# Layer norm 2 normalized by one ScalarE pass, with its weight and bias applied behind the transposes

## The chip, the cores and the metric

The kernel runs on one core of one Trainium2 chip. The metric is the device time of one execution in microseconds (us), lower is better. The engines are named as in the profile: PE (TensorE, with its weight loads PEld), DVE (VectorE), ACT (ScalarE), POOL (GpSimd) and SP (SyncE, which here only issues weight transfers).

## The reference, cut to what matters

Two transformer blocks run one after the other on 256 tokens of width 1024, all in float32. The first block ends in a mixture of experts and a layer norm. The second is two layers of feed-forward, mixer, feed-forward. The change lies on the seam between them:

```python
        ffn = hier_moe(x, w_group[l], b_group[l], w_expert[l], b_expert[l], w_gate_up[l], w_down[l])
        x = layer_norm(DN_ALPHA * x + ffn, ln2_g[l], ln2_b[l])
...
        x = x + FFN_RES_WEIGHT * _swiglu(_rmsnorm(x, ffn1_norm[layer]),
                                         ffn1_w_gate_up[layer], ffn1_w_down[layer])
```

`layer_norm` subtracts each token's mean, multiplies by the reciprocal standard deviation, by the weight `ln2_g` and adds `ln2_b`. `_rmsnorm` divides by the root mean square and multiplies by the gain `ffn1_norm`. The mixer also needs two scalars "lambda", one a layer, each from two dot products of length 64 and an exponential.

## The kernel before, in words

Tokens lie in two tiles of 128 partitions, `t` = 0 and 1, each in two column halves of 512, `hf` = 0 and 1. The order on every engine is the order in which the code is written; an engine works through its list and waits at each instruction for what it needs.

**The experts.** 32 experts go in 8 groups of four (`q` = 0 to 7). SP streams their weights through 10 slots of 1 MB and some more buffers (`Stream`), always ahead of PE. Each group's result is added in PSUM into four banks `yacc[t][hf]`. In the last group `down` leaves `ys`, of which ACT copies one half and DVE the other, and `last` adds it into `yacc`. Between the last `gate_up` and `down` stands `overflow`, a conditional branch that is not entered for these inputs. `gains` (group 6) spreads rows of weights over 128 partitions with small PE products and ACT copies; `lambdas` (group 7) computes the two lambdas.

**LN2 before.** `last_stats(t)` takes `bn_stats` of both halves on DVE, `bn_aggr`, and on POOL the reciprocal standard deviation (L808, L809). `first_norm` then makes on DVE, in two passes over each half, the normalized row with the product of both gains (`ggb`) in it, into `s_xn`. PE transposes it, four 128x128 blocks to a PSUM bank `tp` (`trans_half`, L1362), and `split` makes the two parts that the products need: ACT copies `tp` to `XH` in a rounded format (L300), DVE subtracts to get the rest, `XL` (L301). ACT copies `yacc` to `X` (L1818), which DVE later normalizes with weight and bias for the residual (L813, L814).

**The first feed-forward.** Weights are split the same way by `Feeder`: ACT makes `whi` (L140), DVE `wlo` (L154), in pieces of 1024 columns, each good for two of the eight chunks `k` of the contraction. Every product is three matmuls (`mm3`: L295 with `whi` and `XH`, L296 with `wlo`, L297 with `XL`). The first block, `skew_first`, does token tile 0 (`part(0, k)`), with the transposes of tile 1 between, and then tile 1. From the second block on, a product is for both token tiles at once (256 columns; PSUM tiles `g`, `a`, `o`).

Of the kernel before, what the change touches and what calls it, by code (L numbers as in the profile page):

```python
# [180 lines left out]
def body(tc, A, out, taps=None, stop=None):  # L181
# [3 lines left out]
    with es:  # L185
# [993 lines left out]

        lam = const.tile([128, 2], F32, name="lam")  # L1180
# [8 lines left out]
        def gains():  # L1189
            for c, op in ((0, ALU.mult), (1024, ALU.add)):  # L1190
                for hf in range(2):
                    p = spread(s_ln[32:33, c + hf * 512:c + hf * 512 + 512], 32)
                    for t in range(2):
                        dve.tensor_tensor(X[:, t, hs(hf)], X[:, t, hs(hf)], p, op)
            for a, n in ((s_ln, 4), (s_gg, 2)):
                for i in range(n):
                    act(a[:, hs(i)], spread(a[0:1, hs(i)]), AF.Copy)
            act(aux[:, 512:1024], spread(aux[0:1, 512:1024]), AF.Copy)
            for c in (1, 0):
                pool.tensor_tensor(s_gg[:, c * 1024:(c + 1) * 1024], s_ln[:, c * 1024:(c + 1) * 1024],  # L1200
                                   s_gg[:, 0:1024], ALU.mult)
# [23 lines left out]
        for q in range(NQ):  # L1225
# [5 lines left out]
            def used(c):  # L1231
                for i in gu[c]:
                    st.done(i)
                if q in (CST, CST + 1) and c == 1:
                    st.reserve = 3
                if q == CST + 1 and c == 1:
                    gains()
                if tail and c == 1:
                    scatter(*prev, (0,))
# [11 lines left out]
            if tail:  # L1251
                lambdas()
                s_xn, sA, sB = [st.take() for _ in range(3)]
                overflow(s_xn, sA, sB)
                st.give(sA, sB)
            else:
                way_back(P, q + 1)
                gather(P, 0, q > CST)
# [4 lines left out]
            if q == CST:  # L1263
                s_ln, s_gg, aux = [st.take() for _ in range(3)]
                pool.dma_start(s_ln[0:1, 0:1024], A["ln2_g"])
                pool.dma_start(s_ln[0:1, 1024:2048], A["ln2_b"])
                pool.dma_start(s_ln[32:33, 0:1024], A["ln1_g"])
                pool.dma_start(s_ln[32:33, 1024:2048], A["ln1_b"])
                pool.dma_start(s_gg[0:1, 0:1024], A["ffn1_norm_2"][0:1])
                pool.dma_start(aux[:, 0:512], A["cossin"])  # L1270
                pool.dma_start(aux[0:1, 512:1024], A["lam"])
                pool.dma_start(wr[:, 0:128], A["w_ff"].rearrange("p l n -> p (l n)"))
                pool.dma_start(wr[:, 128:130], A["subln"])
                pool.dma_start(wr[0:8, 130:132], A["fbias"])
                fone = aux[0:8, 1792:2048]
# [4 lines left out]
        ggb = [s_gg[:, c * 1024:(c + 1) * 1024] for c in range(2)]  # L1280
# [10 lines left out]
        def first_norm(t, i):  # L1291

            for hf in range(2):
                dst = s_xn[:, t * 1024 + hf * 512:t * 1024 + (hf + 1) * 512]
                dve.scalar_tensor_tensor(dst, dst if i else yacc[t][hf], mvs[t][:, 3 * i:3 * i + 1],
                                         ggb[i][:, hs(hf)], op0=ALU.mult if i else ALU.subtract,
                                         op1=ALU.add if i else ALU.mult)
# [5 lines left out]
        for i in range(2):  # L1303
            first_norm(0, i)
# [52 lines left out]
        def trans_half(t, hf, src=None):  # L1357
            p = pa("tp")
            src = xn[t] if src is None else src
            for i in range(4):  # L1360
# [3 lines left out]
                  p.rearrange("p (c t) -> p c t", c=4))  # L1364

# [11 lines left out]
        def skew_first(banks, first=False):  # L1377
# [8 lines left out]
            for k in range(4):  # L1386
                part(0, k)
            trans_half(1, 0, xs_[1] if first else None)
            for k in range(4, 8):
                part(0, k)  # L1390
            trans_half(1, 1, xs_[1] if first else None)
            if first:
                for t in range(2):
                    normed(X[:, t], X[:, t], mvs[t], *lnb)
                    stats(t)
            else:
                stats(1)
# [47 lines left out]
        def ffn(g_next, keep_free, first=False, final=False):  # L1445
# [57 lines left out]
            for j in range(NJ):  # L1503
# [3 lines left out]
                if j == 0:  # L1507
                    skew_first(banks, first)
                    if first:
                        st.give(s_ln, s_xn, s_gg)  # L1510
# [294 lines left out]
        xs_ = [s_xn[:, t * 1024:(t + 1) * 1024] for t in range(2)]  # L1805
        fd.hold = True
        fd.hb = 4
        fd.fill()
        fd.flush(1)
        for hf in range(2):  # L1810
            trans_half(0, hf, xs_[0])
        mvs[1] = last_stats(1)
        fd.flush(1)
        for i in range(2):
            first_norm(1, i)
        for t in range(2):
            for hf in range(2):
                act(X[:, t, hs(hf)], yacc[t][hf], AF.Copy)  # L1818
# [17 lines left out]
def host(I):  # L1836
# [3 lines left out]
    A = {}  # L1840
# [37 lines left out]
    A["mrow"] = np.broadcast_to(np.where(dist >= 0, 0.0, -NEG).astype(f), (8, 384))  # L1878
    A["w_rt"] = np.concatenate([I["w_group"][0], I["w_expert"][0]], 1).reshape(8, 128, 36).transpose(1, 0, 2)
# [34 lines left out]
```

## Time and profile before

| | |
|---|---|
| median of 3 runs | 1664.7 us (1662.6 to 1664.9) |
| profiled execution | 1666.04 us, span of the trace 1664.3 us |
| PE busy | 1540.4 us, 93% of the span |
| DVE busy | 819.8 us, 49% |
| ACT busy | 657.3 us, 39% |
| POOL busy | 88.6 us, 5% |
| PE's share of the chain that ended last | 54% |
| mean granted TensorE clock | 0.971 |

The profiled execution lies 1.3 us above the median of the runs, and its span 1.7 us below its own time. Busy shares are averages over stages with different limits: the experts, up to some 665 us, move weights at over 420 GB/s, and behind some 690 us PE is busy nearly all the time. The seam between lies in the two rows of the profile's 40 slices where DMA and PE both have gaps.

### The profile page before, as it was taken

Reading aid. Unit: us, or ns where it says so; the run is one execution under the profiler, and the core shown is the slowest. Engines: PE = TensorE matmul, PEld = TensorE weight load, DVE = VectorE, ACT = ScalarE, POOL = GpSimd, SP = SyncE. Lnnn points to the kernel's source line nnn. Section 1 sums busy time; section 2 is a strip of 40 time slices with the busy share of each in tenths; the row PEclk is TensorE's granted clock in tenths of the full one; section 3 lists DMA queues with packets and bytes.
Section 4 is the critical chain, followed back from the end, with each engine's and each line's share of the span. In section 5 each row is a group of like instructions: output and inputs, shape, how many; then the busy total and the mean of one; then the engine's idle time right before and its main releaser. Section 6 shows DMA issues by size and latency. Waiting matters only on the chain.

```text
span 1664.3 us, 24689 instructions
## 1 busy us (share of the span) xinstructions
PE 1540.4 (93%) x10220; PEld 1201.7 (72%) x10220; DVE 819.8 (49%) x1251; ACT 657.3 (39%) x987; POOL 88.6 (5%) x135
## 2 busy tenths in 40 slices
PE   8999998687677896899999999999999999999998
PEld 7889963122122231699989879999999989889997
DVE  5875640000000100855567865556655568765555
ACT  5556420000000110544445654444544455654442
POOL 3010000000000010100002000000000020000000
PEclk9999999999998798999999999999999999999999
DMA  9757779999999999875614555555555514475500
GB/s 357 195 183 280 279 302 422 422 421 421 421 421 420 419 421 417 318 272 182 203 36 157 206 212 203 200 188 192 190 192 189 176 64 153 178 265 178 200 29 26
DMA packets 85764, 416.49 MB, mean 250 GB/s; under 512 B 7464, under 2 KB 7672, under 8 KB 50320
## 3 DMA queue, kind: packets, MB, share of 16 engines
q1 hardware_dynamic: 82688, 407.07, 64.2%
q0 software_dynamic: 2688, 6.75, 1.4%
q8 instruction: 82, 1.34, 0.3%
q10 hardware_dynamic: 272, 1.05, 0.2%
q14 instruction: 34, 0.28, 0.0%
HBM read 413.56 MB, written 1.25 MB: 249 GB/s over the span
## 4 chain that ended last, share of the span: by engine, by line
PE 54%; DVE 4%; ACT 1%; issue 0%; POOLq 0%; DVEq 0%; POOL 0%; ACTq 0%
PE g L297 8%; PE g L296 8%; PE g L295 8%; PE o L296 5%; PE o L295 5%; PE o L297 5%; PE a L295 4%; PE a L296 3%; PE a L297 3%; DVE wlo L154 1%; PE tp L1362 1%; PE ro L1612 0%; ACT whi L140 0%; PE t L1631 0%; PE fo L469 0%
## 5 line engine op out<-in xcount | busy, mean ns | idle before, releaser
L154 DVE TENSOR_TENSOR wlo<-slot,whi 128x1024 fp32r<-128x1024 f32 x274 | 330.8, 1223 | 202.8 <-ACT whi L140 202.5
L140 ACT ACTIVATE whi<-slot 128x1024 fp32r<-128x1024 f32 x274 | 284.6, 1055 | 223.5 <-PE o L296 69.9
L295 PE MATMUL o<-XH,whi 128*128 128x256 f32 x640 | 177.2, 277 | 0.0
L296 PE MATMUL o<-XL,whi 128*128 128x256 f32 x640 | 177.0, 276 | 0.0
L297 PE MATMUL o<-XH,wlo 128*128 128x256 f32 x640 | 176.9, 276 | 0.0
L295 PE MATMUL g<-whi,OH 128*128 128x512 f32 x416 | 165.2, 397 | 0.0
L297 PE MATMUL g<-whi,OL 128*128 128x512 f32 x416 | 163.9, 394 | 0.0
L296 PE MATMUL g<-wlo,OH 128*128 128x512 f32 x416 | 163.1, 392 | 0.0
L295 PE MATMUL a<-XH,whi 128*128 128x256 f32 x512 | 141.5, 276 | 0.0
L296 PE MATMUL a<-XL,whi 128*128 128x256 f32 x512 | 141.5, 276 | 0.0
L297 PE MATMUL a<-XH,wlo 128*128 128x256 f32 x512 | 141.4, 276 | 0.0
L1070 PE MATMUL eg<-slot,xe 128*32 128x512 f32 x232 | 97.8, 690 | 28.2 <-DMA slot<-in_w_gate_up_dram 28.2
L296 PEld LDWEIGHTS o<-XL,whi 128*128 128x128 f32 x640 | 120.4, 188 | 0.7
L295 PEld LDWEIGHTS o<-XH,whi 128*128 128x128 f32 x640 | 120.1, 188 | 0.7
L297 PEld LDWEIGHTS o<-XH,wlo 128*128 128x128 f32 x640 | 120.2, 188 | 0.0
L1074 DVE TENSOR_TENSOR eb<-eb,eu 128x512 f32<-128x512 f32 x8 | 5.5, 688 | 232.0 <-PE eu L1070 224.0
L295 PE MATMUL g<-XH,whi 128*128 128x256 f32 x384 | 113.9, 297 | 0.0
L297 PE MATMUL g<-XH,wlo 128*128 128x256 f32 x384 | 106.8, 278 | 0.0
L296 PE MATMUL g<-XL,whi 128*128 128x256 f32 x384 | 106.7, 278 | 0.0
L296 PEld LDWEIGHTS a<-XL,whi 128*128 128x128 f32 x512 | 96.2, 188 | 0.7
L295 PEld LDWEIGHTS a<-XH,whi 128*128 128x128 f32 x512 | 96.1, 188 | 0.7
L297 PEld LDWEIGHTS a<-XH,wlo 128*128 128x128 f32 x512 | 96.1, 188 | 0.0
(521 smaller groups left out, 3369.3 us busy)
## 6 DMA issues: line engine op xcount, KB each, us to landing
slot<-in_gu_dram SPq DMA_DIRECT2D x74, 1024.0 KB, 4.9
slot<-in_w_gate_up_dram SPq DMA_DIRECT2D x58, 1024.0 KB, 19.8
slot<-in_w_in_dram SPq DMA_DIRECT2D x36, 1024.0 KB, 5.1
slot<-in_dn_dram SPq DMA_DIRECT2D x34, 1024.0 KB, 4.9
ew<-in_w_down_dram SPq DMA_DIRECT2D x24, 1024.0 KB, 19.8
slot<-in_w_down_dram SPq DMA_DIRECT2D x21, 1024.0 KB, 19.8
ew<-in_w_gate_up_dram SPq DMA_DIRECT2D x16, 1024.0 KB, 19.8
m<-in_w_gate_up_dram SPq DMA_DIRECT2D x13, 1024.0 KB, 19.8
```

Of the source, the lines that this page charges most:

```text
L140: self.nc.scalar.activation(hi[:, c], src[:, c], AF.Copy)
L154: self.low.tensor_tensor(lo[:, c], src[:, c], hi.bitcast(F32)[:, c], ALU.subtract)
L295: mm(o, sh, mh, start=start, stop=False, skip_group_check=skip)
L296: mm(o, sh, ml, start=False, stop=False, skip_group_check=skip)
L297: mm(o, sl, mh, start=False, stop=stop, skip_group_check=skip)
L1070: mm(b[r, :], xe[:, k, r], get(k // 2, e)[:, c:c + 512], start=k == 0, stop=k == 7)
L1074: dve.tensor_tensor(esg, esg, u, ALU.mult)
L1362: nc.tensor.transpose(p[:, i * 128:(i + 1) * 128], src[:, c], ident)
```

## The change

It has five parts. The normalized row is made by ACT alone, from the bank in PSUM straight into `X`, with the reciprocal deviation as scale and minus mean times that as bias (`plain_norm2`; POOL computes the bias, L1293). PE transposes this plain `X`, and weight and bias of LN2, multiplied by the gain of the first RMS norm, are applied behind the transposes, where features lie on partitions (`turn_first`): ACT writes a 128x128 block of `XH`, DVE writes the same block in full to a buffer, four times in turn, and then DVE subtracts. The weights come as `lnc`, 24 columns, and `s_gg` and `s_xn` are gone. The residual's `X` gets weight and bias by plain `tensor_tensor` (L1407). `lambdas` is called from `gains`, one group earlier, and the reserve of slots follows. In `skew_first` the first transposes of tile 1 stand behind six chunks of tile 0 and no longer four; the weight splits are handed out in other steps (`fd.hb` 2, 3, 4).

```diff
-            for c in (1, 0):
-                pool.tensor_tensor(s_gg[:, c * 1024:(c + 1) * 1024], s_ln[:, c * 1024:(c + 1) * 1024],
-                                   s_gg[:, 0:1024], ALU.mult)
+            for c in (0, 8):
+                pool.tensor_tensor(lnc[:, c:c + 8], lnc[:, c:c + 8], lnc[:, 16:24], ALU.mult)
+            lambdas()
...
-                    st.reserve = 3
+                    st.reserve = 2 + q - CST
...
-                lambdas()
-                s_xn, sA, sB = [st.take() for _ in range(3)]
-                overflow(s_xn, sA, sB)
-                st.give(sA, sB)
+                sl = [st.take() for _ in range(3)]
+                overflow(*sl)
+                st.give(*sl)
...
-        def first_norm(t, i):
-
+        def plain_norm2(t):
+
+            mv = mvs[t]
+            pool.tensor_scalar(mv[:, 4:5], mv[:, 0:1], mv[:, 3:4], -1.0, op0=ALU.mult, op1=ALU.mult)
             for hf in range(2):
-                dst = s_xn[:, t * 1024 + hf * 512:t * 1024 + (hf + 1) * 512]
-                dve.scalar_tensor_tensor(dst, dst if i else yacc[t][hf], mvs[t][:, 3 * i:3 * i + 1],
-                                         ggb[i][:, hs(hf)], op0=ALU.mult if i else ALU.subtract,
-                                         op1=ALU.add if i else ALU.mult)
+                act(X[:, t, hs(hf)], yacc[t][hf], AF.Identity, scale=mv[:, 3:4], bias=mv[:, 4:5])
...
-        for i in range(2):
-            first_norm(0, i)
...
+        def turn_first(t, hf):
+
+            p, f = pa("tp"), xn[hf][:, 0:512]
+            for i in range(4):
+                c = 4 * hf + i
+                nc.tensor.transpose(p[:, i * 128:(i + 1) * 128], X[:, t, c * 128:(c + 1) * 128], ident)
+            for i in range(4):
+                c, b = 4 * hf + i, slice(i * 128, (i + 1) * 128)
+                g, b_ = lnc[:, c:c + 1], lnc[:, 8 + c:9 + c]
+                act(XH[:, c, tsl(t)], p[:, b], AF.Identity, scale=g, bias=b_)
+                dve.tensor_scalar(f[:, b], p[:, b], g, b_, op0=ALU.mult, op1=ALU.add)
+            d = slice(4 * hf, 4 * hf + 4)
+            dve.tensor_tensor(XL[:, d, tsl(t)], f.rearrange("p (c t) -> p c t", c=4), XH[:, d, tsl(t)].bitcast(F32),
+                              ALU.subtract)
...
-            for k in range(4):
+            turn = turn_first if first else trans_half
+            n = 6 if first else 4
+            for k in range(n):
                 part(0, k)
-            trans_half(1, 0, xs_[1] if first else None)
-            for k in range(4, 8):
+            turn(1, 0)
+            for k in range(n, 8):
                 part(0, k)
-            trans_half(1, 1, xs_[1] if first else None)
+            turn(1, 1)
             if first:
                 for t in range(2):
-                    normed(X[:, t], X[:, t], mvs[t], *lnb)
+                    for a, op in zip(lnb, (ALU.mult, ALU.add)):
+                        dve.tensor_tensor(X[:, t], X[:, t], a, op)
                     stats(t)
...
-        xs_ = [s_xn[:, t * 1024:(t + 1) * 1024] for t in range(2)]
         fd.hold = True
+        fd.hb = 2
+        fd.fill()
+        fd.flush()
+        plain_norm2(0)
+        turn_first(0, 0)
+        fd.hb = 3
+        fd.fill()
+        turn_first(0, 1)
+        fd.flush()
+        mvs[1] = last_stats(1)
+        plain_norm2(1)
         fd.hb = 4
         fd.fill()
-        fd.flush(1)
-        for hf in range(2):
-            trans_half(0, hf, xs_[0])
-        mvs[1] = last_stats(1)
-        fd.flush(1)
-        for i in range(2):
-            first_norm(1, i)
-        for t in range(2):
-            for hf in range(2):
-                act(X[:, t, hs(hf)], yacc[t][hf], AF.Copy)
         fd.flush()
```

Two places show how the lists of the engines move. First ACT, from the copy of `ys` after the last expert group to the sums of squares (`junk`), before:

```order
L977 ACT_TABLE_LOAD
L977 ACTIVATE ys<-ey 128x512
L140 ACTIVATE whi<-eXL 128x1024 x2
L140 ACTIVATE whi<-slot_69 128x1024 x2
L300 ACTIVATE XH<-tp 128x4x128 x2
L1818 ACTIVATE X<-yacc 128x512 x4
L140 ACTIVATE whi<-slot_70 128x1024 x2
L300 ACTIVATE XH<-tp 128x4x128 x2
L1374 ACTIVATE junk,ss<-X 128x1024 x2
```

and ACT at the same place in the changed kernel (`wr` holds `lnc`, `mv` the statistics):

```order
L977 ACTIVATE ys<-ey 128x512
L140 ACTIVATE whi<-eXL 128x1024 x2
L1295 ACTIVATE X<-yacc,mv 128x512 x2
L1370 ACTIVATE XH<-tp,wr 128x128 x4
L140 ACTIVATE whi<-slot_69 128x1024
L1370 ACTIVATE XH<-tp,wr 128x128 x4
L1295 ACTIVATE X<-yacc,mv 128x512 x2
L140 ACTIVATE whi<-slot_69 128x1024
L140 ACTIVATE whi<-slot_70 128x1024 x2
L1370 ACTIVATE XH<-tp,wr 128x128 x8
L1384 ACTIVATE junk,ss<-X 128x1024 x2
```

The table load ahead of `ys` is gone, `X` of tile 0 now stands ahead of `XH`, each `XH` half is four instructions in place of one, and three weight splits stand between `X` and `XH` of tile 1.

Then DVE, from the first statistics of LN2 to the last `XL` of tile 1, before:

```order
L1288 BN_STATS bst<-yacc 128x6 x2
L807 BN_AGGR mv<-bst 128x2
L1295 SCALAR_TENSOR_TENSOR slot_68<-yacc,mv,slot_72 128x512 x2
L1295 SCALAR_TENSOR_TENSOR slot_68<-slot_68,mv,slot_72 128x512 x2
L154 TENSOR_TENSOR wlo<-eXL,whi 128x1024
L301 TENSOR_TENSOR XL<-tp,XH 128x4x128 x2
```

and DVE at the same place in the changed kernel:

```order
L1287 BN_STATS bst<-yacc 128x6 x2
L807 BN_AGGR mv<-bst 128x2
L154 TENSOR_TENSOR wlo<-eXL,whi 128x1024 x2
L1371 TENSOR_SCALAR xn_3895<-tp,wr 128x128 x4
L1373 TENSOR_TENSOR XL<-xn_3895,XH 128x4x128
L1371 TENSOR_SCALAR xn_3896<-tp,wr 128x128 x4
L1373 TENSOR_TENSOR XL<-xn_3896,XH 128x4x128
L154 TENSOR_TENSOR wlo<-slot_69,whi 128x1024
```

Behind the statistics two weight splits stand at once where the two passes of `first_norm` stood, and each `XL` half now has four reads of the bank `tp` ahead of it; the statistics of tile 1 come a further split later.

## Rows read from the trace of the kernel before

**Rows 1.** Windows: busy time of each engine, granted clock (PEclk), DMA share, GB/s.
```profile
600.00:640.00 40.00, 32.01 (x212) 11.39 (x211) 2.35 (x7) 2.69 (x7) 0.00 (x0) 1.00 1.01 422
```

**Rows 2.** Waits, 692 to 860 us, the only one of PE: us, times, longest.
```profile
PE tp L1362 <- DVE xn L1355: 0.3, 1, 0.3
```

**Rows 3.** Chain that ended last, 666 to 692 us: start, duration, what.
```profile
672.92 1.22 DVE wlo L154
...
677.86 0.72 DVE slot L1295 x2
...
680.51 1.15 DVE wlo L154
```

**Rows 4.** Timeline, 665 to 677 us: start, duration, what, and the idle time before.
```profile
665.26 1.28 ACT L977 ACT_TABLE_LOAD   x1 [12.32 <-PE ey L1092]
...
666.55 0.60 ACT L977 ACTIVATE ys<-ey 128x512 f32<-128x512 f32 x1
...
667.20 3.70 PE L1284 MATMUL yacc<-ys,eb 128*128 128x512 f32 x8 [1.17 <-ACT ys L977]
...
669.96 0.21 DVE L807 BATCH_NORM_AGGREGATE mv<-bst 128x2 f32<-128x12 f32 x1
...
672.48 1.29 PE L1362 MATMUL tp<-cst,slot 128*128 128x128 f32 x8 [1.58 <-DVE slot L1295]
...
675.25 1.28 DVE L1288 BATCH_NORM_STATS2 bst<-yacc 128x6 f32<-128x512 f32 x2
```

**Rows 5.** Timeline of POOL over the whole span.
```profile
670.26 0.22 POOL L808 TENSOR_SCALAR mv<-mv 128x1 f32<-128x1 f32 x1 [81.60 <-DVE mv L807]
...
671.11 0.66 POOL L1332 DMA_DIRECT2D slot<-in_late_dram  x1
676.88 1.08 POOL L808 TENSOR_SCALAR mv<-mv 128x1 f32<-128x1 f32 x1 [5.11 <-DVE mv L807]
...
984.54 1.06 POOL L1369 TENSOR_TENSOR rs<-v,mhalf 128x1 f32<-128x1 f32 x1
```

**Rows 6.** Timeline of DVE, 984 to 986 us.
```profile
984.50 0.69 DVE L1355 TENSOR_TENSOR xn<-X,gain 128x512 f32<-128x512 f32 x1
985.16 1.22 DVE L154 TENSOR_TENSOR wlo<-eXH,whi 128x1024 fp32r<-128x1024 f32 x1
```

**Rows 7.** Timeline of ACT, 215 to 232 us: the plain norm of LN1.
```profile
226.23 1.52 ACT L872 ACTIVATE X<-X,mv 128x512 f32<-128x512 f32 x2 [1.12 <-POOL mv L870]
```

**Rows 8.** Timeline, 228 to 236 us: ACT and DVE in turn on one bank `ga`.
```profile
231.36 0.46 ACT L1006 ACTIVATE xe<-ga,bcol 128x128 f32<-128x128 f32 x1 [3.61 <-PE ga L993]
231.85 0.41 DVE L1004 TENSOR_SCALAR xe<-ga,bcol 128x128 f32<-128x128 f32 x1 [1.80 <-ACT xe L1006]
...
232.29 0.81 ACT L1006 ACTIVATE xe<-ga,bcol 128x128 f32<-128x128 f32 x2 [0.48 <-DVE xe L1004]
```

**Rows 9.** Groups of instructions, 665 to 720 us: count, busy us and mean ns, idle before.
```profile
L154 DVE TENSOR_TENSOR wlo<-slot,whi 128x1024 fp32r<-128x1024 f32 x12 | 13.9, 1220 | 2.3 <-ACT whi L140 2.2
L140 ACT ACTIVATE whi<-slot 128x1024 fp32r<-128x1024 f32 x12 | 11.9, 1049 | 0.3 <-PE g L296 0.3
```

**Rows 10.** Timeline of PE: the first feed-forward block, and the second's first matmul.
```profile
683.14 0.63 PE L296 MATMUL o<-wlo,XH 128*128 128x512 f32 x1
683.57 0.63 PE L297 MATMUL o<-whi,XL 128*128 128x512 f32 x1
...
691.86 0.39 PE L296 MATMUL o<-wlo,XH 128*128 128x512 f32 x1
692.09 0.39 PE L297 MATMUL o<-whi,XL 128*128 128x512 f32 x1
692.32 0.28 PE L295 MATMUL g<-XH,whi 128*128 128x256 f32 x1
```

**Rows 11.** Windows, as Rows 1, in which the granted clock was low.
```profile
679.60:686.20 6.60, 6.02 (x16) 4.58 (x17) 6.05 (x7) 2.60 (x4) 0.10 (x1) 0.51 1.02 407
```

**Rows 12.** Timeline of ACT, 583 to 594 us: first instruction behind `gains`.
```profile
593.98 0.60 ACT L1073 ACTIVATE eb<-eg 128x512 f32<-128x512 f32 x1 [8.48 <-PE eg L1070]
```

More of the change, by code (lines that the diff above doesn't have):

```diff
@@ L1178, in token_weights @@
                 dve.scalar_tensor_tensor(WW[:, t], A1[:, t], rw[:, t, 6:7], WW[:, t], op0=ALU.mult, op1=ALU.add)
+        lnc = wr[:, 260:284]
         lam = const.tile([128, 2], F32, name="lam")
@@ L1194, in gains @@
                         dve.tensor_tensor(X[:, t, hs(hf)], X[:, t, hs(hf)], p, op)
-            for a, n in ((s_ln, 4), (s_gg, 2)):
-                for i in range(n):
-                    act(a[:, hs(i)], spread(a[0:1, hs(i)]), AF.Copy)
+            for i in range(4):
+                act(s_ln[:, hs(i)], spread(s_ln[0:1, hs(i)]), AF.Copy)
             act(aux[:, 512:1024], spread(aux[0:1, 512:1024]), AF.Copy)
-            for c in (1, 0):
-                pool.tensor_tensor(s_gg[:, c * 1024:(c + 1) * 1024], s_ln[:, c * 1024:(c + 1) * 1024],
-                                   s_gg[:, 0:1024], ALU.mult)
+            for c in (0, 8):
+                pool.tensor_tensor(lnc[:, c:c + 8], lnc[:, c:c + 8], lnc[:, 16:24], ALU.mult)
+            lambdas()
         def lambdas():
@@ L1263, in body @@
             if q == CST:
-                s_ln, s_gg, aux = [st.take() for _ in range(3)]
+                s_ln, aux = [st.take() for _ in range(2)]
                 pool.dma_start(s_ln[0:1, 0:1024], A["ln2_g"])
@@ L1268, in body @@
                 pool.dma_start(s_ln[32:33, 1024:2048], A["ln1_b"])
-                pool.dma_start(s_gg[0:1, 0:1024], A["ffn1_norm_2"][0:1])
+                pool.dma_start(lnc, A["lnc"])
                 pool.dma_start(aux[:, 0:512], A["cossin"])
@@ L1279, in body @@
         lnb = [s_ln[:, c * 1024:(c + 1) * 1024] for c in range(2)]
-        ggb = [s_gg[:, c * 1024:(c + 1) * 1024] for c in range(2)]
         bsts = [small.tile([128, 12], F32, name="bst", bufs=2) for _ in range(2)]
@@ L1355, in finish, with trans_half @@
             dve.tensor_tensor(xn[t][:, hs(hf)], xs, g[:, hs(hf)], ALU.mult)
-        def trans_half(t, hf, src=None):
-            p = pa("tp")
-            src = xn[t] if src is None else src
+        def trans_half(t, hf):
+            p, src = pa("tp"), xn[t]
             for i in range(4):
@@ L1364, in trans_half @@
                   p.rearrange("p (c t) -> p c t", c=4))
+        def turn_first(t, hf):
[3 more added lines that the diff above has]
+                nc.tensor.transpose(p[:, i * 128:(i + 1) * 128], X[:, t, c * 128:(c + 1) * 128], ident)
+            for i in range(4):
+                c, b = 4 * hf + i, slice(i * 128, (i + 1) * 128)
[5 more added lines that the diff above has]
+                              ALU.subtract)
         def rms(t, ss):
@@ L1509, in ffn @@
                     if first:
-                        st.give(s_ln, s_xn, s_gg)
+                        st.give(s_ln)
                     turn = first_block()
@@ L1878, in host @@
     A["mrow"] = np.broadcast_to(np.where(dist >= 0, 0.0, -NEG).astype(f), (8, 384))
+    A["lnc"] = np.concatenate([I["ln2_g"][0], I["ln2_b"][0], I["ffn1_norm_2"][0]]).reshape(24, 128).T
     A["w_rt"] = np.concatenate([I["w_group"][0], I["w_expert"][0]], 1).reshape(8, 128, 36).transpose(1, 0, 2)
```

## The prediction

> **What bounds the kernel now.** First the windows of 20 to 40 us, to see which stage waits for what. Until the experts end, the DMA engines are full: between 600 and 640 us their share is 1.01 at 422 GB/s, while PE has 8 us of 40 to spare [rows 1]. So nothing that happens on ACT, DVE or POOL before some 665 us counts, as long as PE is ready when the weights land. Second the waits behind the seam: from 692 to 860 us PE waits 0.3 us in all [rows 2]. So everything behind the first feed-forward block follows at PE's own pace, and the change is worth what it does to the moment at which PE starts the second block, now 692.32 us [rows 10]. Third the chain of waits in the stretch between, to see who holds PE back there: it runs over DVE, in turn the weight splits and the passes of the normalization [rows 3]. The timeline gives the instants: the table load at 665.26, `ys`, `yacc` at 667.20, the end of the statistics at 669.96 and the first transposes at 672.48 [rows 4].
>
> So the question is when the last `XL` of tile 1 is there, since PE needs it for the last four chunks of its first block.
>
> **Lambdas, gains, slots.** `lambdas` moves into group 6, with a table load ahead of its exponentials and one back, twice 1.28 us. ACT had been idle for 8.48 us at the first instruction behind `gains` [rows 12], and the DMA engines bound that stage: nothing. If ACT's gap were gone, these would still have to outlast PE's spare time [rows 1]. The spreads and the long product left out of `gains`, and the slots, lie in the same stage: nothing.
>
> **The table load** of 1.28 us ahead of `ys` falls away, and `yacc` waited for `ys` with PE idle [rows 4]. `ys` starts at 665.26 and `yacc` at 665.95; the DVE half, done at 666.8, is needed no earlier. Statistics end at 668.75 + 0.2 = 668.9, **1.2 us earlier**. The Trainium skill ("ScalarE: Activation LUTs", What ACT_TABLE_LOAD costs) puts a change of tables at 1.28 us for the load and as much again for a drain, about 2.7. Here `ys` began 0.01 us behind the load's end [rows 4], so the trace shows no such second part; by the page the sum below would come out 1.4 us lower.
>
> **POOL now stands in the path.** Before, DVE could begin its first pass with the mean alone. Now `X` needs L808, L809 and L1293 from POOL, and the DMA issue of `late` (L1332), which stands ahead of L1293. Alone these take 0.22, 0.57 (estimated from the gap to the next row), 0.66 and 0.22 as another L808 [rows 5]. But the DVE now starts two weight splits at once behind the statistics. At 676.88 the same L808 beside a split took 1.08 in place of 0.22, and at 984.54 a small POOL operation took 1.06 beside DVE's two-operand passes [rows 5, 6]. So I hold L808 to the end of the first split (668.9 + 1.2 = 670.1) and L809 to the end of the second (671.2) plus 0.5, which makes 671.7; the issue ends at 672.4, L1293 at 672.6. `X` starts at **672.7**. Bound below: nothing is held, 670.8, which is 1.9 earlier; I take the held one, as it is the nearest row.
>
> **Tile 0.** One `X` half takes 1.52 / 2 = 0.76 [rows 7], four transposes 1.29 / 2 = 0.65 [rows 4]; the first `XH` block starts at 674.25, when ACT is through with the second half of `X`.
>
> **Taking turns in the bank.** ACT and DVE read the same blocks of `tp` by turns, and in the changed program's order each waits for the other's last read. The trace has this pattern in the gather, on `ga`: ACT at 231.36, DVE at 231.85 behind it, the next ACT at 232.29 behind that, each 0.41 to 0.46 long, with the releaser named [rows 8]. A pair costs 232.29 - 231.36 = 0.93. Four blocks take 3 x 0.93 + 0.49 + 0.41 = 3.69, and the subtraction, two operands in SBUF, 0.69 as L1355 [rows 6], 4.4 with the step between. Before, the half was one ACT copy and one subtraction. `XL` half 0 ends at **678.7**. ACT puts one `whi` of 1.0 between [rows 9], starts the second half at 678.6, and DVE ends `XL` at **683.05**.
>
> **Tile 1.** DVE: a split 1.15 [rows 3], two statistics 1.28, their sum 0.21 [rows 4]: 685.65. POOL, no longer beside a split, 0.22 + 0.57 + 0.22 and three steps between engines, together 1.35: `X` starts at 687.0 and ends at 688.5. Now ACT has three `whi` ahead of its first `XH` (some 1.0 each [rows 9]): 691.5. DVE has the three `wlo` that go with them, the last from 691.85 to 693.0. From there two halves by turns: 693.0 + 2.79 + 0.41 + 0.05 + 0.69 = 697.0, and the same again, 4.0 more: the last `XL` at **700.95**.
>
> **PE's rest.** Behind this `XL` stand ten products of the first block (one of chunk 4, three each of chunks 5 to 7) at 692.09 - 691.86 = 0.23 each [rows 10]: the second block starts at 703.3 and not 692.3, **+11.0**. Of the clock: in the stretch before, from 679.6 to 686.2, the granted clock was 0.51, the lower of the two levels (1.2 of 2.4 GHz), and a product took 683.57 - 683.14 = 0.43 [rows 10, 11]. It came behind a stretch in which PE had waited; the change makes PE wait more and later, so such a stretch may lie on the last products. At 6.6 us of half speed this costs 0 to 3.3 more; ten products at 0.43 would be 2.0; I take 1.3. DVE is also later with the splits of the second block, since four passes over `X` follow the last `XL`: +0.2.
>
> Sum: 11.0 + 1.3 + 0.2 = **+12.5**. The profiled execution took 1666.04, so 1678.5; it lies 1.3 above the median, so the forecast is 1664.7 + 12.5 = **1677.2 us**. A difference of 0.2%, 3.3 us, is about what a measurement of this kernel can tell from none.
>
> **Rivals.**
>
> *Turns cost less.* If both engines read the bank side by side, a half takes 4 x 0.46 + 0.41 = 2.25 and not 3.69; four halves save 5.8. That gives +6.7, **1671.4**. Against it: both idle times in the gather name the other engine [rows 8]. The Trainium skill ("PSUM — Partial Sum Buffer", PSUM bank collisions raise a hardware error) says that two engines must be kept from one bank and quadrant by semaphores, reads too; the gather's rows agree, and by it this case would not occur. Chance 0.06.
>
> *It evens out.* The same, with POOL not held (-1.9) and the clock at its upper level (-1.3): +3.5, half of it within 0.2%, **1667**. Chance 0.05.
>
> *Faster: DVE's own work decides.* If ACT, POOL and PE are always ready, DVE's list counts alone: from 668.9 two splits 2.3, sixteen reads 6.6, four subtractions 2.8, four more splits 4.6, statistics 1.5; that is 17.8, so the last `XL` is at 686.7, PE's block ends at 689.0, -3.3: **1661.4**. For it speaks that DVE makes the chain now [rows 3] and loses eight passes of normalization. The point from which it decides: the forecast has 14 us of DVE idle in that stretch (700.95 - 686.7), and this case needs under 3. Against it: the turns alone leave DVE idle 0.53 a block (0.93 less 0.41), 8 us, and the three `whi` and POOL come on top. Chance 0.05.
>
> **How the numbers follow.** Forecast 0.84, from +9 (POOL free, clock up) to +15 (clock down for longer): 1673.7 to 1679.7, with the spread of the runs on either side 1672 to 1681. The range reaches to the cases below, 1669 to 1682. Slower has the forecast, the cheaper turns, and half of the evened case: 0.91 with rounding, same 0.04, faster 0.05.
>
> **What would show it.** In the changed profile: no table load at 665; L808 and L809 each over 1 us beside the splits; L1370 and L1371 in turn, 0.93 a pair, each released by the other; the last L1373 of tile 1 near 701; the first `g` matmul near 703 to 705 and all behind it merely shifted, with no new wait of PE. Wrong would be the forecast if DVE shows no gaps between the reads, if the second block starts before 696, or if the time is lost in the expert stage, where I put nothing.

## The result, and the profile after

The changed kernel takes **1676.3 us** (median of 4 runs, 1674.9 to 1676.8) against 1664.7 before: the ratio is 1.0068, 95% interval 1.0056 to 1.0081, so it is slower by 11.6 us. The forecast was 1677.2. The profiled execution took 1676.82 us, 10.78 more than that of before, with a span of 1675.0. Medians here and below are of executions at the usual speed; three executions of later kernels, each 100 us or more above the others of its kernel, are left out.

First the timeline of the changed kernel from the end of the experts to the reads of the first transposed bank, with POOL's part for tile 1 (start, duration, what, and the idle time before with its releaser):

```profile
666.82 0.60 ACT L977 ACTIVATE ys<-ey 128x512 f32<-128x512 f32 x1 [14.83 <-PE ey L1092]
...
670.27 0.21 DVE L807 BATCH_NORM_AGGREGATE mv<-bst 128x2 f32<-128x12 f32 x1
...
670.58 0.22 POOL L808 TENSOR_SCALAR mv<-mv 128x1 f32<-128x1 f32 x1 [118.15 <-DVE mv L807]
670.67 2.36 DVE L154 TENSOR_TENSOR wlo<-eXL,whi 128x1024 fp32r<-128x1024 f32 x2 [0.19 <-issue]
670.88 1.45 POOL L809 TENSOR_TENSOR mv<-mv,mhalf 128x1 f32<-128x1 f32 x1
...
672.30 0.66 POOL L1328 DMA_DIRECT2D slot<-in_late_dram  x1
...
673.05 0.26 POOL L1293 TENSOR_SCALAR mv<-mv 128x1 f32<-128x1 f32 x1
673.34 1.45 ACT L1295 ACTIVATE X<-yacc,mv 128x512 f32<-128x512 f32 x2 [3.71 <-POOL mv L1293]
...
674.91 0.46 ACT L1370 ACTIVATE XH<-tp,wr 128x128 fp32r<-128x128 f32 x1
...
675.46 0.41 DVE L1371 TENSOR_SCALAR xn<-tp,wr 128x128 f32<-128x128 f32 x1 [2.43 <-issue]
...
675.91 0.46 ACT L1370 ACTIVATE XH<-tp,wr 128x128 fp32r<-128x128 f32 x1 [0.54 <-DVE xn L1371]
...
676.40 0.41 DVE L1371 TENSOR_SCALAR xn<-tp,wr 128x128 f32<-128x128 f32 x1 [0.53 <-ACT XH L1370]
...
676.85 0.46 ACT L1370 ACTIVATE XH<-tp,wr 128x128 fp32r<-128x128 f32 x1 [0.48 <-DVE xn L1371]
...
678.72 0.69 DVE L1373 TENSOR_TENSOR XL<-xn,XH 128x512 fp32r<-128x512 f32 x1
...
686.51 0.58 POOL L809 TENSOR_TENSOR mv<-mv,mhalf 128x1 f32<-128x1 f32 x1
```

There is no table load ahead of `ys` any more [rows 4]. POOL's L809 takes 1.45 us where it begins just behind the start of a split, two and a half times its 0.58 for tile 1, where no split runs beside it, and the DMA issue stands between it and L1293. Then ACT and DVE read one bank by turns: each is released by the other, and from one `XH` to the next it is 676.85 - 675.91 = 0.94 us, as in the gather before [rows 8].

Then the chain of waits of the changed kernel towards the end of the stretch, where before it ran over splits and passes of DVE [rows 3]:

```profile
695.64 0.47 ACT XH L1370
696.13 0.42 DVE xn L1371
696.57 0.69 DVE XL L1373
...
700.44 0.70 DVE XL L1373
```

The turns of L1371 and L1370 are the two largest lines of this chain between 664 and 712 us (12.8% and 12.4% by its own count). The last `XL` of tile 1 ends at 701.13, and PE has ten products of its first block left. The first matmul of the second block, which was at 692.32 [rows 10], is here (timeline of PE):

```profile
701.18 0.50 PE L297 MATMUL o<-whi,XL 128*128 128x512 f32 x1 [0.83 <-DVE XL L1373]
...
703.37 0.40 PE L297 MATMUL o<-whi,XL 128*128 128x512 f32 x1
703.60 0.28 PE L295 MATMUL g<-XH,whi 128*128 128x256 f32 x1
```

The step between the last products is 0.23 us (703.60 - 703.37), and the granted clock was 1.00, its upper level. I call **the seam** the time from the last expert product, where ACT can begin with `ys` (its table load before), to this matmul. Before it took 692.32 - 665.26 = 27.06 us, now 703.60 - 666.82 = 36.78: 9.72 more. The rest of the difference lies on both sides of it. From this matmul to the last product of the program it was 964.18 us (1656.50 - 692.32) and is 963.73: 0.45 less. And the experts end 1.56 us later in this execution, on which the windows of the two profiles tell more (us, PE busy, granted clock, DMA share, GB/s), before:

```profile
640.00:644.00 4.00, 2.55 (x12) 0.72 1.01 420
644.00:648.00 4.00, 4.00 (x24) 0.85 1.02 426
```

and changed:

```profile
640.00:644.00 4.00, 2.56 (x10) 0.66 1.01 422
644.00:648.00 4.00, 4.00 (x21) 0.50 1.01 422
```

The DMA engines are as full as in [rows 1], but the last gate and up products meet the lower clock up to the end of this window and not for part of it only. (changed_again below shows what else moves this end from one profile to the next.) So 1.56 + 9.72 - 0.45 = 10.83, close to the 10.78 of the profiled executions.

### The profile page after: what moved, and what is told of

Read it like the earlier page. It is cut to its first block, busy times and chain, and to the rows that moved or that the text cites. A ratio compares the mean times of both kernels' runs of the same rounds, so it can differ in the third digit from the quotient of the medians.

```text
span 1675.0 us, 24692 instructions
## 1 busy us (share of the span) xinstructions
PE 1543.3 (92%) x10216; PEld 1201.6 (72%) x10216; DVE 821.0 (49%) x1259; ACT 660.1 (39%) x996; POOL 84.7 (5%) x137
## 3 DMA queue, kind: packets, MB, share of 16 engines
HBM read 413.56 MB, written 1.25 MB: 248 GB/s over the span
## 4 chain that ended last, share of the span: by engine, by line
PE 63%; DMA 26%; DVE 6%; ACT 2%; issue 1%; POOL 1%; SPq 0%; POOLq 0%; DVEq 0%; ACTq 0%
PE g L297 10%; PE g L295 10%; PE g L296 10%; DMA slot<-in_w_gate_up_dram 6%; PE o L297 5%; PE o L296 5%; PE o L295 5%; DMA slot<-in_w_down_dram 5%; PE a L296 4%; PE a L295 4%; PE a L297 4%; DMA m<-in_w_gate_up_dram 4%; DMA ew<-in_w_gate_up_dram 4%; DMA e<-in_w_down_dram 2%; DMA ew<-in_w_down_dram 2%; DVE wlo L154 1%
## 5 line engine op out<-in xcount | busy, mean ns | idle before, releaser
L1070 PE MATMUL eg<-slot,xe 128*32 128x512 f32 x228 | 102.4, 700 | 28.4 <-DMA slot<-in_w_gate_up_dram 28.4
```

The source lines that it names most:

```text
L1070: mm(b[r, :], xe[:, k, r], get(k // 2, e)[:, c:c + 512], start=k == 0, stop=k == 7)
```

## The experiments

Eleven kernels ran. Medians are compared with the kernel before in the same session (1664.1 to 1664.4 us); as the end of the experts wanders between the profiles (below), the seam of the profiled execution is given beside each time.

| kernel | median, us | ratio to before, 95% interval | last expert product, us | seam, us |
|---|---|---|---|---|
| before | 1664.7 | | 665.26 | 27.06 |
| changed | 1676.3 | 1.0056 to 1.0081 | 666.82 | 36.78 |
| changed_again | 1676.7 | 1.0060 to 1.0089 | 665.70 | 37.73 |
| two_banks | 1667.4 | 1.0013 to 1.0030 | 662.19 | 30.64 |
| act_then_dve | 1670.8 | 1.0028 to 1.0053 | 666.17 | 31.45 |
| lambdas_back | 1676.3 | 1.0058 to 1.0084 | 666.80 | 38.71 |
| splits_later | 1675.8 | 1.0060 to 1.0086 | 664.41 | 34.67 |
| lambdas_alone | 1663.3 | 0.9986 to 1.0004 | 663.83 | 26.42 |
| stats_first | 1671.4 | 1.0028 to 1.0053 | 665.85 | 34.41 |
| two_banks_stats_first | 1665.1 | 0.9990 to 1.0011 | 667.51 | 26.91 |
| x1_between | 1670.3 | 1.0025 to 1.0049 | 664.08 | 31.95 |
| two_banks_x1_between | 1662.3 | 0.9973 to 0.9991 | 663.80 | 24.43 |
| one_split_first | 1662.4 | 0.9983 to 1.0001 | 665.76 | 24.34 |

**Two banks.** PE transposes each half twice, and each engine has a bank of its own (`pg` takes the banks of `yacc` as they come free):

```diff
             p, f = pa("tp"), xn[hf][:, 0:512]
-            for i in range(4):
-                c = 4 * hf + i
-                nc.tensor.transpose(p[:, i * 128:(i + 1) * 128], X[:, t, c * 128:(c + 1) * 128], ident)
+            p2 = pg("tq")
+            for pp in (p, p2):
+                for i in range(4):
+                    c = 4 * hf + i
+                    nc.tensor.transpose(pp[:, i * 128:(i + 1) * 128], X[:, t, c * 128:(c + 1) * 128], ident)
...
-                dve.tensor_scalar(f[:, b], p[:, b], g, b_, op0=ALU.mult, op1=ALU.add)
+                dve.tensor_scalar(f[:, b], p2[:, b], g, b_, op0=ALU.mult, op1=ALU.add)
```

> The changed kernel with one edit: PE transposes each half of the plain X twice, into two banks, ACT reads the one and DVE the other, so that neither waits for the other's reads. Theory (the turns in one bank cost 0.94 us a block): a half falls from 3.7 us to some 2.0 (four steps of 0.40 and one of 0.41), four halves save 6.8 us, the second set of transposes gives 0.7 back where it is on the path: 5 to 6.5 us faster than the changed kernel, 1670 to 1671.5 us. Rival (the reads are slow by themselves, or POOL and the splits set the pace): less than 1.5 us faster, above 1674.5 us.

The timeline of two_banks, the first half of tile 0:

```profile
670.28 1.50 ACT L1372 ACTIVATE XH<-tp,wr 128x128 fp32r<-128x128 f32 x4
...
670.73 1.37 DVE L1373 TENSOR_SCALAR xn<-tq,wr 128x128 f32<-128x128 f32 x4 [2.33 <-PE tq L1368]
...
672.20 0.69 DVE L1375 TENSOR_TENSOR XL<-xn,XH 128x512 fp32r<-128x512 f32 x1
```

Four blocks now take 1.50 us on ACT and 1.37 on DVE, side by side, and from the first `XH` to the end of `XL` it is 2.61 us (672.89 - 670.28) where the changed kernel has 4.50 (679.41 - 674.91). The seam falls by 6.1 us, inside what the theory gave. The last `XL` itself comes 7.45 us earlier behind the last product (26.86 us, from 688.36 + 0.69 - 662.19, and not 34.31); PE's products, at the lower clock up to some 688 us, give 1.3 of it back. The time falls by 8.9, more than the seam. Part of that may be the experts, which ended early in this kernel's profile (below); the medians can't tell the parts apart, so I credit the edit with the seam only.

**ACT first, then DVE**, in one bank:

```diff
-            for i in range(4):
-                c, b = 4 * hf + i, slice(i * 128, (i + 1) * 128)
-                g, b_ = lnc[:, c:c + 1], lnc[:, 8 + c:9 + c]
-                act(XH[:, c, tsl(t)], p[:, b], AF.Identity, scale=g, bias=b_)
-                dve.tensor_scalar(f[:, b], p[:, b], g, b_, op0=ALU.mult, op1=ALU.add)
+            blk = [(4 * hf + i, slice(i * 128, (i + 1) * 128)) for i in range(4)]
+            for c, b in blk:
+                act(XH[:, c, tsl(t)], p[:, b], AF.Identity, scale=lnc[:, c:c + 1], bias=lnc[:, 8 + c:9 + c])
+            for c, b in blk:
+                dve.tensor_scalar(f[:, b], p[:, b], lnc[:, c:c + 1], lnc[:, 8 + c:9 + c], op0=ALU.mult, op1=ALU.add)
```

> The changed kernel with one edit: in each half ACT reads all four blocks of the bank and only then DVE reads them, so one hand-over in place of seven, the same instructions. Theory (the hand-overs between the engines cost, and the two may not read at once): a half takes 4 x 0.40 + 4 x 0.36 + 0.1 = 3.1 us in place of 3.75, four halves 2.5 us, so some 1674 us. Rival (the hand-overs are free, only the reading times count): no change, 1676.3 us.

The timeline of act_then_dve, both halves of tile 0:

```profile
674.54 1.51 ACT L1369 ACTIVATE XH<-tp,wr 128x128 fp32r<-128x128 f32 x4 [0.40 <-ACT X L1295]
...
676.14 1.37 DVE L1371 TENSOR_SCALAR xn<-tp,wr 128x128 f32<-128x128 f32 x4 [3.76 <-issue]
...
677.54 0.69 DVE L1373 TENSOR_TENSOR XL<-xn,XH 128x512 fp32r<-128x512 f32 x1
...
679.82 0.69 DVE L1373 TENSOR_TENSOR XL<-xn,XH 128x512 fp32r<-128x512 f32 x1
```

The same sixteen pairs of instructions, in another order, and the seam is 5.3 us shorter, twice what I had expected. I had counted the saving within a half only. But ACT, done with its bank, makes its split and reads the second half's bank while DVE reads the first: the two `XL` of tile 0 end 5.97 us behind the first `XH` (680.51 - 674.54) where it is 8.60 in the changed kernel (683.51 - 674.91). So the cost lies in the turns, not in the reading: the same instructions read the same bank. One bank read in blocks by one engine and then the other does nearly as well as two banks.

**Lambdas back in the last group:**

```diff
-            lambdas()
...
             if tail:
+                lambdas()
                 sl = [st.take() for _ in range(3)]
```

> The changed kernel with lambdas called in the last expert group again, as before the change. Theory (the table load of 1.28 us ahead of ys lay on the path): the load comes back between the last expert product and ys, 1.2 to 1.3 us slower than the changed kernel, 1677.5 us. Rival (the last product came 1.6 us later because of what lambdas does in group 6): the last product comes back to 665.3 us, and the time is the same or up to 0.3 us less, 1676.0 us. Third: the later product comes from the lower clock of PE in the last gate and up products, which does not depend on lambdas: then the products stay late and the load is added, 1677.6 us.

The table load stands ahead of `ys` again, and the statistics' sum comes 4.70 us behind the last product (671.50 - 666.80), where it is 3.45 in the changed kernel: 1.25 of the seam's 1.93. The last product is as late as without the edit (666.80, 666.82), as the third case has it. One profile of each is thin, since this end wanders; but the ten profiles below that have the changed code ahead of it give 665.2 us in the mean, against before's 665.26, so nothing shows that moving `lambdas` delays it. In the time the table load does not show: the medians, of 5 and 4 runs, lie within 0.1 us, and its price is below what the wandering experts let one see.

**Two splits later:**

```diff
             turn(1, 1)
             if first:
+                fd.hb = HB3
+                fd.fill()
...
         fd.hold = False
-        fd.hb = HB3
-        fd.fill()
```

> The changed kernel with two of the three weight splits that stand ahead of tile 1's reads (those for the second block) moved behind them. Theory (they lie on the path): DVE's first read of tile 1 comes 2.2 us earlier, the second block starts 2 us earlier, some 1674.2 us, if the second block finds its splits in time. Rival (they only fill time in which tile 1 waits anyway, or the second block then waits for them): no change within 0.5 us, or slower.

The last `XL` begins 31.52 us behind the last product (695.93 - 664.41) where it was 33.62 (700.44 - 666.82), and the seam falls by 2.1, as expected. But the four passes over `X` now stand behind these two splits on DVE (from 698.81 us), ACT's sums of squares wait for the passes, and ACT's next splits stand behind the sums, up to 704.83 us. The waits of PE in splits_later behind 699 us show what came of it:

```profile
PE g L295 <- ACT whi L140: 1.2, 1, 1.2
PE g L297 <- DVE wlo L154: 0.8, 1, 0.8
```

The second block waits 2.0 us for a pair of splits, and part of the stretch behind ran at a lower clock (0.76 in the mean from 705 to 712 us). The rest of the program takes 967.22 us and not 963.73: more than the seam saved is given back. The theory is right for the seam, the rival for the whole.

**Lambdas alone**, on the kernel before:

```diff
                 pool.tensor_tensor(s_gg[:, c * 1024:(c + 1) * 1024], s_ln[:, c * 1024:(c + 1) * 1024],
                                    s_gg[:, 0:1024], ALU.mult)
+            lambdas()
...
-                lambdas()
                 s_xn, sA, sB = [st.take() for _ in range(3)]
```

> The kernel before with one part of the change alone: lambdas called from gains in group 6. Theory (the table load lay between the last expert product and yacc, nothing else there changes): from the last product to the first matmul of the second feed-forward block 1.3 us less than before's 27.06 us, some 25.8; in the time 1.3 us less, 1662.8 us, plus or minus what the end of the experts wanders. Rival (the load was covered): 27.0 us.

The timeline of lambdas_alone:

```profile
663.83 0.60 ACT L977 ACTIVATE ys<-ey 128x512 f32<-128x512 f32 x1 [14.68 <-PE ey L1092]
...
667.28 0.21 DVE L807 BATCH_NORM_AGGREGATE mv<-bst 128x2 f32<-128x12 f32 x1
...
669.80 1.29 PE L1362 MATMUL tp<-cst,slot 128*128 128x128 f32 x8 [1.58 <-DVE slot L1295]
...
672.79 1.09 ACT L300 ACTIVATE XH<-tp 128x512 fp32r<-128x512 f32 x2 [3.16 <-SPq L1104]
672.84 0.82 SPq L86 DMA_DIRECT2D slot<-in_gu_dram  x2
```

The statistics' sum comes 3.45 us behind the last product, 1.25 less than before (669.96 - 665.26 = 4.70), and the transposes follow. But then `XH` waits 3.16 us for SP's conditional branch (L1104), which releases it at the moment at which SP goes on issuing. Only 0.64 of the seam is saved, and the time is the same within its interval. (A low-clock stretch also lies in another place here, from some 672 to 682 us and not from 679 to 686, so the wait need not be all of the difference.) Before, the first `XH` (673.19 us) stood just behind that moment (672.60) and hid it. I had not seen this wait; in the changed kernel SP goes on at 670.31, ahead of the first `XH`.

**The changed kernel again**, unedited:

> The changed kernel without any edit, run once more. Theory (the end of the experts wanders with the low-clock stretches of PE from one execution to the next, while the seam behind it is the same): from the last expert product to the first matmul of the second block 36.8 us within 0.8, while the last product itself ends anywhere from 662 to 667 us. Rival (the end of the experts belongs to the kernel): the last product at 666.8 us within 0.3 again.

The last product comes at 665.70 and not at 666.82 with the same kernel, so its instant does not belong to the kernel alone. Over the thirteen profiles it lies between 662.19 and 667.51; ten of them have the same code ahead of it, and their mean is 665.2. I had put this down to the clock, but the profiles show three things that differ. The granted clock is one, as above. The arrival of the weights is another: the last gate and up products that wait for them begin anywhere from 640.96 us (two_banks) to 644.23 (two_banks_stats_first). The third is the conditional branch `overflow` on PE, first in before, then in two_banks (the instructions of L1104: ns of the one branch, and when):

```profile
L1104 PEldq COMPARE_BRANCH  x1: 6072/6072/6072, 648.8 to 648.8; - x1
...
L1104 PEldq COMPARE_BRANCH  x1: 450/450/450, 647.4 to 647.4; - x1
```

It took 5.8 to 6.2 us in ten profiles, and 0.45, 0.45 and 0.85 in two_banks, splits_later and two_banks_x1_between. Whether that goes with the kernel or with the execution no run shows.

The seam is 37.73, 0.15 outside what I allowed. Of the 0.95 more, 0.46 lie on the first transposes, which ran at the lower clock (the first `XH` starts 8.55 us behind the last product and not 8.09), and 0.47 on a low-clock stretch over products from 696.7 to 700.2.

**Statistics first:**

```diff
-            return moments(bsts[t])
+            mv = moments(bsts[t])
+            pool.tensor_scalar(mv[:, 4:5], mv[:, 0:1], mv[:, 3:4], -1.0, op0=ALU.mult, op1=ALU.mult)
+            return mv
...
-        mvs = [last_stats(0), None]
+        mvs = [last_stats(0), last_stats(1)]
...
         plain_norm2(0)
+        plain_norm2(1)
         turn_first(0, 0)
...
-        mvs[1] = last_stats(1)
-        plain_norm2(1)
```

> The changed kernel with the statistics of tile 1 right behind those of tile 0, the bias of both on POOL ahead of the DMA issue, and X of tile 1 made right behind X of tile 0. Theory (POOL held beside the splits and the DMA issue cost some 1.5 us, and the statistics, POOL and the X of tile 1 stand on the chain for 5 us, with ACT's splits behind them): L808 and L809 take 0.22 and 0.57, X of tile 0 starts some 1.5 us earlier, DVE's first read of tile 1 some 6 us earlier; the seam takes 31 us in place of 36.8, so some 1670.5 us. Rival (only the turns count): 1 us or less is saved.

The timeline of stats_first:

```profile
669.30 0.21 DVE L807 BATCH_NORM_AGGREGATE mv<-bst 128x2 f32<-128x12 f32 x1
...
669.91 0.57 POOL L809 TENSOR_TENSOR mv<-mv,mhalf 128x1 f32<-128x1 f32 x1
...
670.89 1.45 ACT L1296 ACTIVATE X<-yacc,mv 128x512 f32<-128x512 f32 x2 [2.23 <-POOL mv L1289]
...
671.42 2.36 DVE L154 TENSOR_TENSOR wlo<-eXL,whi 128x1024 fp32r<-128x1024 f32 x2 [0.19 <-issue]
671.62 1.45 POOL L809 TENSOR_TENSOR mv<-mv,mhalf 128x1 f32<-128x1 f32 x1
...
671.72 1.32 PE L1367 MATMUL tp<-cst,X 128*128 128x128 f32 x8 [1.47 <-ACT X L1296]
...
673.95 1.45 ACT L1296 ACTIVATE X<-yacc,mv 128x512 f32<-128x512 f32 x2 [1.61 <-POOL mv L1289]
...
675.29 0.46 ACT L1371 ACTIVATE XH<-tp,wr 128x128 fp32r<-128x128 f32 x1
```

The price of POOL beside the splits is right: beside `bn_stats` L809 takes 0.57, beside the splits the same instruction 1.45, and `X` of tile 0 starts 1.59 us behind the statistics' sum and not 3.07. But the seam falls by 2.4 only. POOL's hold has moved to tile 1: ACT waits for it at `X` of tile 1 (673.95) while the first bank of tile 0 lies ready at 672.4, and `XH` begins at 675.29. A low-clock stretch lay on the products of the first block too, up to 698.3 us (0.43 us from one to the next).

**X of tile 1 between the halves**, on top of that:

```diff
         plain_norm2(0)
-        plain_norm2(1)
         turn_first(0, 0)
+        plain_norm2(1)
```

> stats_first with one edit: X of tile 1 is made behind the first half of XH of tile 0 and no longer ahead of it. Theory (stats_first gave back what it saved because ACT stood at X of tile 1, which waits for POOL held beside the splits, while the first bank was ready for 2.9 us): XH of tile 0 starts as soon as its bank is ready, DVE's first read comes 2 us earlier, X of tile 1 costs 0.7 of it between the halves: the seam takes some 33.1 us in place of 34.4, give or take 1.5 for the clock of the last products. Rival (POOL has no part in it): no change of the instant of the first XH against the first transposes.

`XH` starts at the first transposes' end (669.94, 670.68) and the seam is 31.95, 2.5 less, where the forecast had 1.3. The last `XL` comes only 0.83 us earlier behind the last product (29.49 and not 30.32); the other 1.63 are the clock of the last products, at its upper level here.

**Both together**, two banks with the statistics first:

> Both edits of two_banks and stats_first on the changed kernel. Theory (the two costs lie one behind the other): 6.1 and 6 us off 36.8, the seam takes some 24.7 us and so 2.4 less than before's 27.06: some 1662 us, at most as slow as before. Rival (PE itself, with transposes done twice and 48 products, or DVE's list sets a floor): the seam stays above 27 us and the time above 1664 us.

The seam is 26.91, level with before, and so is the time, 0.9990 to 1.0011 of it. What it still loses, as the next kernel shows, are the 3 us for which ACT stands at `X` of tile 1.

**And with X of tile 1 between:**

> two_banks_stats_first with the same edit. Theory: XH of tile 0 starts 3 us earlier (676.95 to some 674.0 where the last expert product is at 667.51), then DVE's two splits are the last to end, so 1.7 us of it reach the end: the seam takes some 25.2 us, 1.9 less than before's 27.06, some 1663 us. Rival (PE's own products at the lower clock set the end): the seam stays at 26.5 to 27 us and the time at 1665.

The timeline of two_banks_x1_between:

```profile
670.46 1.51 ACT L1373 ACTIVATE XH<-tp,wr 128x128 fp32r<-128x128 f32 x4 [0.17 <-PE tp L1369]
...
673.11 0.69 DVE L1376 TENSOR_TENSOR XL<-xn,XH 128x512 fp32r<-128x512 f32 x1
...
684.41 0.69 DVE L1376 TENSOR_TENSOR XL<-xn,XH 128x512 fp32r<-128x512 f32 x1
...
688.23 0.28 PE L295 MATMUL g<-XH,whi 128*128 128x256 f32 x1
```

The seam is 24.43 us, 2.6 less than before, and the kernel takes 1662.3 us, ratio 0.9982 (0.9973 to 0.9991): faster than before, clear of its interval, by 2.1 us. The last `XL` ends at 685.1, and PE works without a gap from 678 us to the second block, so DVE no longer sets its end alone. That this profile has one of the short branches on PE does not make the gain: the next kernel has a long one (5.97 us) and much the same time.

**One split first**, on top:

```diff
         fd.fill()
-        fd.flush()
+        fd.flush(1)
         plain_norm2(0)
         turn_first(0, 0)
+        fd.flush(1)
         plain_norm2(1)
```

> two_banks_x1_between with one of the two splits that stand ahead of DVE's first reads moved behind the first half. Theory (those splits are what DVE's first reads wait for): XL of the first half 1.1 us earlier, the seam some 24.2 us, some 1662 us. Rival (PE's products set the end): no change against two_banks_x1_between.

The timeline of one_split_first:

```profile
671.32 1.23 DVE L154 TENSOR_TENSOR wlo<-eXL,whi 128x1024 fp32r<-128x1024 f32 x1 [0.19 <-issue]
671.52 1.45 POOL L809 TENSOR_TENSOR mv<-mv,mhalf 128x1 f32<-128x1 f32 x1
...
684.94 0.50 PE L297 MATMUL o<-whi,XL 128*128 128x512 f32 x1 [0.46 <-DVE XL L1376]
```

The seam is 24.34 and the time 1662.4: no change, as the rival has it. Its reason is not shown, though: in this execution PE still waits 0.46 us for an `XL` of tile 1, and its clock is at the upper level throughout the seam. The first half's `XL` of tile 0 comes earlier (9.21 us behind the last product and not 10.00, from 674.28 + 0.69 - 665.76 and 673.11 + 0.69 - 663.80), but the second half's only 0.10 (12.51 and 12.61), since the split that was moved now stands ahead of it.

## Why the prediction was right

The mechanism was right, and the size was near, partly by luck; the steps one by one, each from the profiled executions.

- *The stretch decides.* From 720 to 860 us PE is busy all 140 us, and only 0.45 us of the difference lies behind the seam. Right.
- *Lambdas, gains, slots.* Nothing was forecast, and nothing shows that they cost anything: the experts' end is at 665.2 us in the mean of ten profiles with them moved, and at 665.26 in the one of before.
- *The table load.* 1.2 us were forecast; the statistics' sum comes 1.25 earlier behind the last product, in the change, in lambdas_alone and (the other way) in lambdas_back. Right. The Trainium skill ("ScalarE: Activation LUTs", What ACT_TABLE_LOAD costs) counts a drain of as much again; the runs differ, since 1.25 is the load's 1.28 alone. What the step left out is what the 1.2 us would be worth by themselves: without the rest of the change, half of it is lost again, by the profile mainly to SP's branch.
- *POOL.* From the start of the statistics' sum to `X` I counted 3.95 us (672.7 - 668.75); it took 3.07 (673.34 - 670.27). L808 slipped in ahead of the first split (0.22 and not 1.2), and L809 was held to the end of the first split only: it ended at 672.33, 0.48 behind it (the pair took 2.36 from 670.67, so the first ended at 671.85), while the second ran on to 673.03. In one_split_first, where one split stands there and not two, L809 takes the same 1.45. The held value was nearer than the free one, but it is one hold and not two.
- *Turns.* From the first `XH` to the first `XL`'s end 4.45 were forecast (678.7 - 674.25) and 4.50 measured; for the second half 4.35 and 4.10; for the two halves of tile 1 7.95 and 7.72. Two experiments remove the turns in different ways and take 6.1 and 5.3 us off the seam. Shown. Where the Trainium skill ("PSUM — Partial Sum Buffer", PSUM bank collisions raise a hardware error) asks for an order by semaphores between readers of one bank, two_banks agrees from the other side: in banks of their own the two engines read side by side.
- *Tile 1's statistics and splits.* From the second `XL` to `X` of tile 1 3.95 forecast, 3.98 measured; from there to the end of the third split 6.0 and 5.92. (The two lists of DVE under The change stop at tile 0; the statistics, splits and reads of tile 1 follow them.)
- *PE's rest.* Ten products, 2.35 forecast and 2.47 measured.
- *The clock* of the last products, 1.3 forecast, was 0 in the profiled execution of the change and 0.47 in changed_again.
- *Behind the seam* 0.2 were forecast for late splits; it was 0.45 less and not more.
- *The experts.* Nothing was forecast, and the profiled execution lost 1.56 us there, with the clock at its lower level for longer.

So of the 12.5 the seam's steps were 1.3 too much (11.0 and 9.72; POOL's 0.9 is most of it), the clock's 1.3 did not come, and behind the seam it was 0.65 less than forecast. Against that stand 1.56 us of the experts, which makes the 10.8 of the profiled execution. That the time came so near to the forecast (11.6 us more, and 12.4 for changed_again in its own session) is luck to this extent: a wandering end of the experts, where I had put nothing, stood in for a clock that did not fall. What the medians hold beyond the seam is not taken apart by any run. The rival in which turns cost less falls by the rows of L1370 and L1371, each released by the other. The rival in which DVE's own work decides shows what would have made the change a gain: in two_banks_x1_between, with the turns gone and POOL's waits shorter and better placed, it is one, of 2.1 us; its 3.3 was not reached.

Open is what places the low-clock stretches. They lie behind stretches in which PE had gaps, but not behind all of them: in one_split_first PE was idle for 4.5 of the 24 us from 666 to 690, and the granted clock stayed at 1.00. They differ from one execution to the next, and no experiment here was made to move them. Open is also what makes PE's branch short or long. That SP's branch is what `XH` waits for in lambdas_alone rests on the profile's releaser and on the instant at which SP goes on issuing; no run took the branch away.

## What to carry to other kernels

Where two engines read one PSUM bank by turns, a pair of short instructions costs the sum of both and two hand-overs; let one engine read all of it and then the other, or give each a bank, before counting on them side by side. A step that moves work off a busy engine is worth what the new round trip costs: here ACT's pass needed three POOL instructions beside DVE's splits, and a reordering of the statistics cut the time from their sum to `X` of tile 0 from 3.07 to 1.59 us. And a wait that is removed in front of one resource can be taken by the next, as the table load's was, by the profile, by a branch: look at what else becomes ready at that moment.

## What the runs showed of the hardware

- A POOL instruction of 128 elements that begins beside a DVE pass with two operands in SBUF takes longer and ends behind that pass: L809 took 1.45 us and not 0.57, and ended 0.48 behind the first split, not behind the second that followed at once. Beside `bn_stats`, which reads PSUM, it took 0.57.
- The same code ends its expert stage anywhere from 662.2 to 667.5 us over ten profiles. Between the profiles of before and of the change, the last gate and up products that wait for weights begin within 0.01 us of each other (642.28 and 642.29), and what differs is how long the granted clock stays at the lower of its two levels (0.50) on them. Over all profiles the arrival of those weights (640.96 to 644.23) and a conditional branch on PE (0.45 to 6.2 us) differ too. A change of 2 us behind such a stage is read from the stretch itself, not from one run's time.
- Instructions of 128 x 128 that follow one another on the same engine cost 0.38 us on ACT (1.50 for four) and 0.34 on DVE; in turns each costs 0.46 and 0.41, and the hand-over 0.03 to 0.04 more.
